# A hybrid decoder layer on eight cores: more staging buffers for x, earlier sample-cache loads, residual loads on another queue, and a narrower last token piece

## The chip, the cores and the metric

The kernel runs on all 8 cores of one Trainium2 chip. Each core computes half of one prompt (1024 tokens, with 128 tokens of halo in front) and 4 of the 32 sample tokens. The cores do not talk to each other. Times are device microseconds (us) of the slowest core.

Most executions of one kernel agree within 0.3%. Some executions fall in a slow state, in which one die (cores 0 to 3, or 4 to 7) runs at a lower granted TensorE clock and takes some per cent longer, whatever the kernel. All comparisons below use fast executions alone, and so do the medians unless their row says otherwise.

## The reference, cut to what matters

```python
# D_MODEL 2048, 4 prompts x 2048 tokens, 32 sample tokens, one layer
h = rms_norm(x, norm_mix_g)
z = h @ w_in                                  # q | k | v | conv value | conv gate
q = rope(rms_norm(q)); k = rope(rms_norm(k))
a = sliding_window_attention(q, k, v)         # window 128; sample tokens read cache_k, cache_v
u = u_val * sigmoid(u_gate)
c = silu(layer_norm(causal_dwconv(u)))
x = x + concat(a, c) @ w_out                  # "residual": x is read again here
hm = rms_norm(x, norm_mlp_g)
x = x + square(relu(hm @ w_up)) @ w_down      # hidden 8192
```

## The kernel before

Five engines work side by side: PE (matmuls), DVE and ACT (elementwise work and reading results out of PSUM), POOL and SP (these mostly issue loads). Activations lie transposed: 128 features on the partitions, tokens along the free dimension. There are 1028 real tokens on a core (1024 prompt and 4 sample), padded to `NM = 1032` and cut into three pieces of 344 columns (`PM`), so that a matmul covers 344 columns.

Every operation goes through a helper (`mm`, `tt`, `ts`, `act`, `cp`, `dma`), and each helper is one source line in the profile. In the kernel before, L613 is a matmul, L577 a DVE tensor-tensor operation, L590 a DVE scaling, L573 an ACT activation, L595 an ACT copy and L560 a load. With the change, all these numbers are higher by 3. The helper records dependencies. At build time `P.schedule()` then fixes the order on each engine with a simple model, taking program order as the priority. At run time each engine works strictly in its order.

The stages, with their times on core 0, are: x and the key/value projection (0 to 56 us), statistics, k, v and q (to 134 us), the convolution inputs with attention between them (to about 310), the output projection with the convolution's layer norm inside it (to about 440), and the MLP (to the end).

The start. x comes in 16 chunks of 128 features:

```python
XST = [sb(O_A + 16384 + 4640 * i, F32, (HW,)) for i in range(4)]       # 4 staging buffers
xd = []
for kc in range(16):
    xs_ = XST[kc % 4]
    xd.append(dma("sp", xs_(), R(xt_d[kc]), "xst%d" % (kc % 4)))
    dma("pool", WKV(kc), R(wkv_d[kc]), "wkv%d" % kc, after=[xd[max(kc - 3, 0)]] if kc >= 2 else [])
    if kc == 6:                      # loads of the rotary tables
        dma("sp", CSE(), R(cse_d), "cse", after=[xd[3]])
        dma("sp", TB(p=(0, 32)), R(tab_d...), "tab", after=[xd[3]])
    if kc == 10:                     # six times: PE spreads a table piece, ACT copies it out
        cp("act", BD(), CSE((0, 128)))
        cp("act", GQK(), CSE((256, 260)))
        for j, tb in enumerate((COS, SIN)):
            for a, b in ((0, 388), (388, 776), (776, 1160)):
                pb = ps_f32(7, 1, (b - a,))
                P.group()
                mm(pb(), CSE((128, 256), p=(0, 32)), TB(j, (a, b), p=(0, 32)), True, True)
                cp("act", tb((a, b)), pb())
    ts("dve", HT(kc), xs_(), G1(kc), ALU.mult)          # DVE: scale the chunk
    act(SQX[kc % 2](), xs_(), AF.Square)                # ACT: square it (chunk 0: into SS1 itself)
    if kc >= 2:
        tt("dve", SS1(), SS1(), SQX[(kc - 1) % 2](), ALU.add)   # DVE: sum the squares
    # PE: 10 matmuls of keys and values with this chunk
```

The sample caches are loaded on POOL's queue after the first of eight convolution channels, and the next convolution weights (`wu`) follow on the same queue:

```python
for c in range(8):
    # ... six groups of matmuls for channel c, attention between them
    if c == 0:
        gate_s = [P.streams["pe"][-1]]
        dma("pool", KTS((0, SPC), (0, 2), (0, 127)), R(ckt), "cks", group=True, after=gate_s)
        dma("pool", CVB(p=(0, 127)), R(cv[:, 1:128, :].rearrange("s k d -> k s d")), "cks", ...)
    if c == 4:
        gate_xt = [P.streams["pe"][-1]]
    for _ in range(2):
        ... wu.append(wstream(wu_d[order[wnext]], "wu", 128))
```

The output projection adds each result to a residual chunk `XT(dc)`. All residual loads are on SP's queue, and 12 of them wait for the last convolution channel:

```python
def xt_load(dc):
    dma("sp", XT(dc), R(xt_d[dc][:, MC0:MC0 + NM]), "xt%d" % dc, after=gate_xt)

def wo_half(dc, half, src):
    ...
    for kc in range(8):
        for pi, (a, b) in enumerate(PM):
            mm(accb(pi, (0, PW)), lw, src(kc, (a, b)), kc == 0, kc == 7)
    tt("dve", x3(), accb((0, 3), (0, PW)), x3(), ALU.add)

gate_xt = [u4_last]
for dc in range(4, 16):
    xt_load(dc)
...
for dc in range(6, 16):                    # first half of the projection, with the
    wo_half(dc, 0, AT)                     # convolution's layer norm between
    if dc - 6 < 8:
        ln_chunk(dc - 6)                   # two DVE operations and one ACT operation
for dc in range(16):                       # second half, and the square for the next norm
    wo_half(dc, 1, CT)
    norm2(dc)
```

In the last column block of the down-projection, the three token pieces of one accumulation finish together and are then added and stored one after the other:

```python
for i in range(n):
    for pi, (a, b) in enumerate(PM):
        mm(accb(pi, (0, PW)), wd[i](dc), hid(i % GFF, (a, b)), i == 0, i == n - 1)
if last and dc == 15:
    for pi, (a, b) in enumerate(PM):
        tt("dve", x3(pi), accb(pi, (0, PW)), x3(pi), ALU.add)
        dma("sp", R(yt[...]), XT(dc, (a, min(b, NO))), ...)
```

## Time and profile before

| | before |
|---|---|
| time, median of 6 runs, one of them slow | 1352.19 us (1349.49 to 1595.09) |
| span of cores 0 to 7 in the profile | 1350.0, 1340.4, 1342.8, 1345.9, 1345.3, 1347.0, 1339.4, 1344.4 us |
| end of DVE's last scaling of x (A), mean of cores | 57.2 us (54.3 to 60.4) |
| start of the convolution inputs on PE (B), mean | 135.5 us |
| from B to the start of the last PE group (E), mean | 1150.4 us |
| from E to the end, mean | 58.5 us |

A, B and E are marks that I set in the timelines of all eight cores. E is the last row of PE's timeline, which starts a new row after an idle time of over 0.15 us; it is the same matmul in every run, the 362nd from the end.

The head of the page gives the span and the busy time of each engine, with its share of the span:

```profile
span 1350.0 us, 22872 instructions; the slowest of 8 cores (1339.4 to 1350.0 us)
PE 1310.1 (97%) x9253; PEld 842.0 (62%) x9253; DVE 702.1 (52%) x853; ACT 290.6 (22%) x441; POOL 111.4 (8%) x199
```

PE is the bound. The chain of waits of core 0 (start, length, what) shows the steady state of the MLP, 384 matmuls in 56.25 us, or 146.5 ns per matmul of 344 columns:

```profile
507.28 56.25 PE psum L613 x384
...
563.56 56.26 PE psum L613 x384
```

Gains can therefore only come from places where PE idles or runs at a low clock, and from narrower matmuls. There are three such places.

*The start.* The table by stretches of core 0 has the columns: stretch and its length, then busy time and number of instructions of PE, PE weight loads, DVE, ACT and POOL, then granted clock, DMA share and GB/s.

```profile
40.00:44.00 4.00, 4.00 (x10) 1.53 (x10) 0.66 (x2) 2.12 (x3) 0.31 (x1) 0.50 0.71 182
44.00:48.00 4.00, 2.78 (x16) 1.34 (x14) 4.00 (x5) 2.66 (x3) 0.53 (x1) 0.80 0.79 184
48.00:52.00 4.00, 3.33 (x21) 1.81 (x20) 4.00 (x5) 1.95 (x3) 0.86 (x2) 1.00 0.92 266
```

From 40 to 44 us the DMA engines are busy only 0.71 of the time, and DVE works only 0.66 of 4 us. The timelines of ACT (first line) and DVE (the others) on core 0 show why; the bracket is the idle time before an instruction and what ended it:

```profile
41.88 0.48 ACT L595 COPY arena<-psum 128x384 f32<-128x384 f32 x1 [3.36 <-PE psum L613]
...
38.09 1.37 DVE L577 TENSOR_TENSOR arena<-arena 128x1160 f32<-128x1160 f32 x1 [3.60 <-ACT arena L573]
43.53 1.37 DVE L577 TENSOR_TENSOR arena<-arena 128x1160 f32<-128x1160 f32 x1 [3.34 <-ACT arena L573]
...
54.86 0.82 DVE L590 TENSOR_SCALAR arena<-arena 128x1160 bf16<-128x1160 f32 x1
```

ACT's copy of a rotary table piece waits for PE, whose chunk matmuls ahead of the table matmul run at clock 0.5. ACT's next square stands behind that copy, and DVE's sum waits for the square. Call this the table stall. After 43.53 us DVE runs without a wait, 2.01 us a chunk.

*The sample caches.* POOL's timeline on core 0 shows the issues, and the view of one tile the time from issue to landing, first for the value cache (`cv`), then for the convolution weights (`wu`):

```profile
152.12 0.89 POOL L560 DMA_DIRECT2D arena<-ckt  x1 [7.70 <-PE psum L613]
153.00 4.58 POOL L560 DMA_DIRECT2D arena<-cv  x1
157.57 0.56 POOL L560 DMA_DIRECT2D arena<-wu  x1
```

```profile
DMA to landing us min/median/max: 31.4/31.4/31.4
...
DMA to landing us min/median/max: 6.1/7.7/29.4
```

The value cache lands 31.4 us after its issue, and the weights behind it take 29.4 us instead of 7.7. The table by stretches (same columns) shows PE standing still, and then working at half clock:

```profile
184.00:186.00 2.00, 0.00 (x0) 0.00 (x0) 0.00 (x0) 0.00 (x0) 0.00 (x0) 0.88 0.84 166
186.00:188.00 2.00, 0.76 (x3) 0.43 (x4) 0.00 (x0) 0.00 (x0) 0.00 (x0) 0.50 0.41 73
188.00:190.00 2.00, 2.00 (x8) 1.03 (x7) 0.00 (x0) 0.00 (x0) 0.00 (x0) 0.50 0.45 109
```

*The residual.* On core 0 the timelines of DVE and PE show a long wait for x, and the wait of PE that it causes:

```profile
341.36 1.23 DVE L577 TENSOR_TENSOR arena<-psum,arena 128x1032 f32<-128x1032 f32 x1 [12.27 <-DMA arena<-xt]
...
343.98 23.86 PE L613 MATMUL psum<-arena 128*128 128x344 f32 x132 [5.63 <-DVE arena L577]
368.76 922.74 PE L613 MATMUL psum<-arena 128*128 128x344 bf16 x6292 [0.91 <-DVE arena L577]
```

No other core has this wait in the profiled execution.

*The end* costs little. On core 0 three additions follow PE's last matmuls in one piece of 1.36 us:

```profile
1344.46 1.36 DVE L577 TENSOR_TENSOR arena<-psum,arena 128x344 f32<-128x344 f32 x3 [1.98 <-PE psum L613]
```

### The profile page before, as it was taken

To read this page: it belongs to the slowest core of one execution; us is meant where nothing else is said; L and a number is where in the kernel's file an instruction comes from. 1 tells how busy PE (TensorE), PEld (TensorE's weight loads), DVE (VectorE), ACT (ScalarE), POOL (GpSimd) and SP (SyncE) were. 2 spreads that over 40 slices of the span, in tenths; PEclk is the share of its full clock that TensorE was granted. 3 is DMA by queue.
4 is the path that set the end of the run, shared out by engine and by line. 5 is a ranking of instruction groups with operands and counts; after the bars stand their busy time and mean duration, and the time that the engine had idled before them with its cause. 6 is when DMAs were issued, how large, how long until landed. Compare 5 with 4: busy or idle time off the path is not lost.

```text
span 1350.0 us, 22872 instructions; the slowest of 8 cores (1339.4 to 1350.0 us)
## 1 busy us (share of the span) xinstructions
PE 1310.1 (97%) x9253; PEld 842.0 (62%) x9253; DVE 702.1 (52%) x853; ACT 290.6 (22%) x441; POOL 111.4 (8%) x199
## 2 busy tenths in 40 slices
PE   5999989999899999999999999999999999999998
PEld 2566545555466666666666666666666666666665
DVE  4666746664676335436354363543635436354333
ACT  3655646562246310000100001000010000100000
POOL 2300200000011110010000101001010010100000
PEclk9899989999899999999999999999999999999999
DMA  9990545655847693351734517335163451624123
GB/s 239 180 161 5 62 99 107 149 112 112 222 73 121 120 158 56 69 94 32 137 58 71 94 32 137 58 72 94 32 135 59 72 94 32 126 53 73 17 106 146
DMA packets 57667, 130.58 MB, mean 97 GB/s; under 512 B 19108, under 2 KB 22692, under 8 KB 57508
## 3 DMA queue, kind: packets, MB, share of 16 engines
q0 software_dynamic: 38880, 90.74, 40.2%
q1 hardware_dynamic: 18684, 38.38, 9.4%
q8 instruction: 75, 1.23, 0.4%
q14 instruction: 28, 0.23, 0.1%
HBM read 202.31 MB, written 10.35 MB: 158 GB/s over the span
## 4 chain that ended last, share of the span: by engine, by line
PE 90%; DMA 6%; DVE 1%; SPq 1%; issue 1%; ACT 0%; POOL 0%; DVEq 0%; ACTq 0%; POOLq 0%
PE psum L613 90%; DMA arena<-xt 2%; DMA arena<-wu 2%; DVE arena L577 1%; SPq L877 1%; DMA arena<-wkv 1%; DMA arena<-arena 0%; POOL arena L560 0%; ACT arena L573 0%; DVE arena L590 0%; SPq L560 0%; ACT arena L595 0%; DVEq L384 0%; DVEq L374 0%; ACTq L374 0%
## 5 line engine op out<-in xcount | busy, mean ns | idle before, releaser
L613 PE MATMUL psum<-arena 128*128 128x344 bf16 (+6 forms) x9253 | 1310.1, 316 | 34.5 <-DMA arena<-wkv 15.1
L613 PEld LDWEIGHTS psum<-arena 128*128 128x128 bf16 (+2 forms) x9253 | 842.0, 99 | 502.3 <-issue 91.4
L577 DVE TENSOR_TENSOR arena<-psum,arena 128x1032 f32<-128x1032 f32 (+7 forms) x367 | 385.0, 1060 | 283.0 <-PE psum L613 263.5
L577 DVE TENSOR_TENSOR arena<-arena 128x516 bf16<-128x516 bf16 (+13 forms) x431 | 305.4, 735 | 343.5 <-ACT arena L573 325.9
L573 ACT ACTIVATE arena<-psum 128x512 bf16<-128x512 f32 (+8 forms) x173 | 124.6, 739 | 819.4 <-PE psum L613 809.1
L573 ACT ACTIVATE arena<-arena 128x352 f32<-128x352 f32 (+9 forms) x194 | 138.7, 730 | 90.2 <-DVE arena L577 70.8
L560 POOL DMA_DIRECT2D arena<-wup x64 | 33.8, 529 | 391.8 <-PE psum L613 391.8
L560 POOL DMA_DIRECT2D arena<-wdn x64 | 33.9, 529 | 384.7 <-PE psum L613 383.8
L573 ACT ACTIVATE arena<-psum,arena 128x344 f32<-128x344 f32 (+6 forms) x58 | 31.8, 575 | 68.7 <-PE psum L613 68.7
L590 DVE TENSOR_SCALAR arena<-arena 128x1160 bf16<-128x1160 f32 (+2 forms) x25 | 18.9, 756 | 13.2 <-DMA arena<-xt 12.2
L560 POOL DMA_DIRECT2D arena<-wo x16 | 11.3, 704 | 136.8 <-PE psum L613 136.8
L560 POOL DMA_DIRECT2D arena<-wu x16 | 8.5, 532 | 141.3 <-PE psum L613 138.4
L560 POOL DMA_DIRECT2D arena<-wkv x16 | 9.1, 567 | 35.0 <-DMA arena<-xt 34.1
L560 POOL DMA_DIRECT2D arena<-wq x16 | 9.1, 614 | 8.3 <-DMA arena<-xt 8.3
L573 ACT ACT_TABLE_LOAD x3 | 3.8, 1283 | 8.8 <-DMA arena<-xt 7.4
L595 ACT COPY arena<-psum 128x388 f32<-128x388 f32 (+1 forms) x6 | 2.9, 481 | 11.1 <-PE psum L613 11.1
L560 POOL DMA_DIRECT2D arena<-cv x1 | 4.6, 4576 | 0.0
L597 DVE COPY arena<-arena 128x4 f32<-128x4 f32 (+1 forms) x11 | 3.8, 356 | 0.4
L605 POOL MEMSET arena<- 128x32 f32 x1 | 0.1, 124 | 42.6 <-PE psum L613 42.6
L590 DVE TENSOR_SCALAR arena<-psum 128x388 bf16<-128x388 f32 (+1 forms) x3 | 1.7, 560 | 1.9 <-PE psum L613 1.8
L601 DVE TENSOR_REDUCE arena<-arena 128x4 f32<-128x124 f32 x8 | 2.2, 278 | 0.5
L595 ACT CAST arena<-arena 128x128 bf16<-128x128 f32 (+2 forms) x6 | 1.5, 300 | 0.5 <-DMA arena<-cse 0.5
(9 smaller groups left out, 3.8 us busy)
## 6 DMA issues: line engine op xcount, KB each, us to landing
arena<-wdn POOLq DMA_DIRECT2D x64, 512.0 KB, 9.4
arena<-wup POOLq DMA_DIRECT2D x64, 512.0 KB, 6.1
arena<-xt SPq DMA_DIRECT2D x16, 580.0 KB, 9.1
arena<-arena SPq DMA_DIRECT2D x128, 65.8 KB, 4.0
arena<-xt SPq DMA_DIRECT2D x16, 516.0 KB, 17.7
arena<-wu POOLq DMA_DIRECT2D x16, 512.0 KB, 7.7
arena<-wo POOLq DMA_DIRECT2D x16, 512.0 KB, 7.1
yt<-arena SPq DMA_DIRECT2D x15, 514.0 KB, 3.9
```

Of the source, the lines that this page charges most:

```text
L560: return P.add(eng, lambda e: e.dma_start(out=out.ap, in_=in_.ap), reads=[in_], writes=[out], key=key, group=group, final=final, after=aft ...
L573: return P.add("act", lambda e: e.activation(out=out.ap, in_=in_.ap, func=func, bias=b, scale=s), reads=rd, writes=[out], cost=cost("act", ...
L577: return P.add(eng, lambda e: e.tensor_tensor(out=out.ap, in0=in0.ap, in1=in1.ap, op=op), reads=[in0, in1], writes=[out], cost=cost(eng, o ...
L590: return P.add(eng, lambda e: e.tensor_scalar(out=out.ap, in0=in0.ap, scalar1=a, scalar2=b, op0=op0, **kw), reads=rd, writes=[out], cost=c ...
L595: return P.add("act", lambda e: e.copy(out=out.ap, in_=in_.ap), reads=[in_], writes=[out], cost=cost("act", out, [in_]))
L597: return P.add(eng, lambda e: e.tensor_copy(out=out.ap, in_=in_.ap), reads=[in_], writes=[out], cost=cost(eng, out, [in_]))
L601: return P.add("dve", lambda e: e.tensor_reduce(out=out.ap, in_=in_.ap, axis=AX.X, op=ALU.add), reads=[in_], writes=[out], cost=(size(in_) ...
L605: return P.add(eng, lambda e: e.memset(out.ap, val), writes=[out], cost=cost(eng, out, []))
L613: return P.add("pe", lambda e: e.matmul(out.ap, lhsT.ap, rhs.ap, start=start, stop=stop), reads=[lhsT, rhs], writes=[out], cost=c)
L877: last = P.add("sp", (lambda src=src, dst=dst: (lambda e: e.dma_start(out=dst.ap, in_=src.ap)))(), reads=[src], writes=[u4()] if i == 0 el ...
```

## The change

It has five parts. (1) x gets eight staging buffers, with six loads in flight, so that its loads run ahead through the table stall. (2) The sample caches are loaded while q is computed, ahead of the convolution. (3) Twelve of the residual loads go to ACT's queue and are issued one by one in step with the output projection, whose column order changes to fit. (4) The last token piece has 340 columns instead of 344. (5) The last column block of the down-projection finishes its token pieces one after the other.

```diff
+PN = [(0, 344), (344, 688), (688, 1028)]
-    XST = [sb(O_A + 16384 + 4640 * i, F32, (HW,)) for i in range(4)]
+    XST = ([sb(O_A + 16384 + 4640 * i, F32, (HW,)) for i in range(4)]
+           + [sb(O_E + 9280 + 4640 * i, F32, (HW,)) for i in range(2)]
+           + [sb(O_G + 4640 + 4640 * i, F32, (HW,)) for i in range(2)])
@@ loop over the chunks of x
-        xs_ = XST[kc % 4]
-        xd.append(dma("sp", xs_(), R(xt_d[kc]), "xst%d" % (kc % 4)))
-        dma("pool", WKV(kc), R(wkv_d[kc]), "wkv%d" % kc, after=[xd[max(kc - 3, 0)]] if kc >= 2 else [])
+        xs_ = XST[kc % 8]
+        xd.append(dma("sp", xs_(), R(xt_d[kc]), "xst%d" % (kc % 8), after=[xd[kc - 6]] if kc >= 6 else []))
+        dma("pool", WKV(kc), R(wkv_d[kc]), "wkv%d" % kc, after=[xd[max(kc - 4, 0)]] if kc >= 2 else [])
@@ before the q projection
+    wu_d3 = P.streams["pool"][-1]
@@ after it (and removed from "if c == 0" of the convolution loop)
+    gate_s = [wu_d3]
+    dma("pool", KTS((0, SPC), (0, 2), (0, 127)), R(ckt), "cks", group=True, after=gate_s)
+    dma("pool", CVB(p=(0, 127)), R(cv[:, 1:128, :]...), "cks", group=True, after=gate_s)
@@ output projection
-        dma("sp", XT(dc), R(xt_d[dc][:, MC0:MC0 + NM]), "xt%d" % dc, after=gate_xt)
+        dma("sp" if dc < 4 else "act", XT(dc), R(xt_d[dc][:, MC0:MC0 + NM]), "xt%d" % dc, after=gate_xt)
-    gate_xt = [u4_last]
-    for dc in range(4, 16):
-        xt_load(dc)
+    DCO = list(range(4)) + list(range(8, 16)) + list(range(4, 8))
+    gate_xt = []
+    xt_more(3)                       # three loads ahead
+    ... xt_more(n): issues the next n residual loads, in the order of DCO
+    def wo_first(i):
+        wo_half(DCO[i], 0, AT)
+        gate_xt = [P.streams["pe"][-1]]
+        xt_more(1)                   # one more after each column block
@@ all large matmuls after attention
-            for pi, (a, b) in enumerate(PM):
-                mm(accb(pi, (0, PW)), lw, src(kc, (a, b)), kc == 0, kc == 7)
+            for pi, (a, b) in enumerate(PN):
+                mm(accb(pi, (0, b - a)), lw, src(kc, (a, b)), kc == 0, kc == 7)
@@ down-projection
+            if last and dc == 15:
+                steps = [(i, pi) for pi in range(3) for i in range(n)]
... (weight pairs, norm2 and the up-projection follow the new order and width)
```

More of the change, by code (lines that the diff above doesn't have):

```diff
@@ L824, in build_program @@
     dma("sp", FS((0, 8), (0, SPC), (0, 30)), R(sct), "fs", after=[wqd[15]])
+    gate_s = [wu_d3]
+    dma("pool", KTS((0, SPC), (0, 2), (0, 127)), R(ckt), "cks", group=True, after=gate_s)
+    dma("pool", CVB(p=(0, 127)), R(cv[:, 1:128, :].rearrange("s k d -> k s d")), "cks", group=True, after=gate_s)
+    for s in range(SPC):
+        dma("sp", CVB(s, p=(127, 128)), VB_S(p=(s, s + 1)), "cvs", group=True)
     CC = sb(O_B, F32, (8, NM))
@@ L975, in build_program @@
     wo2 = []
+    PAIRS = [0, 1, 4, 5, 6, 7, 2, 3]
     def wo_load(half, pair):
@@ L997, in build_program @@
         u4_last = u_done(c)
-        if c == 0:
-            gate_s = [P.streams["pe"][-1]]
-            dma("pool", KTS((0, SPC), (0, 2), (0, 127)), R(ckt), "cks", group=True, after=gate_s)
-            dma("pool", CVB(p=(0, 127)), R(cv[:, 1:128, :].rearrange("s k d -> k s d")), "cks", group=True, after=gate_s)
-            for s in range(SPC):
-                dma("sp", CVB(s, p=(127, 128)), VB_S(p=(s, s + 1)), "cvs", group=True)
         if c == 4:
@@ L1010, in build_program @@
             else:
-                wo2.append(wo_load(0, len(wo2)))
+                wo2.append(wo_load(0, PAIRS[len(wo2)]))
     dma("sp", R(uf_d), Ref(UF.ap.rearrange("p a b -> p (a b)"), UF().rngs), "uf", final=True)
@@ L1015, in xt_load @@
     def xt_load(dc):
-        dma("sp", XT(dc), R(xt_d[dc][:, MC0:MC0 + NM]), "xt%d" % dc, after=gate_xt)
+        dma("sp" if dc < 4 else "act", XT(dc), R(xt_d[dc][:, MC0:MC0 + NM]), "xt%d" % dc, after=gate_xt)
     for dc in range(4):
         xt_load(dc)
-    wo_left = [(0, p) for p in range(len(wo2), 8)] + [(1, p) for p in range(8)]
+    wo_left = [(0, p) for p in PAIRS[len(wo2):]] + [(1, p) for p in PAIRS]
     def wo_half(dc, half, src):
@@ L1062, in build_program, with xt_more @@
     conv_sums(6)
-    gate_xt = [u4_last]
-    for dc in range(4, 16):
-        xt_load(dc)
-    for dc in range(3):
-        wo_half(dc, 0, AT)
+    DCO = list(range(4)) + list(range(8, 16)) + list(range(4, 8))
+    xt_next = [4]
+    def xt_more(n):
+        for _ in range(n):
+            if xt_next[0] < 16:
+                xt_load(DCO[xt_next[0]])
+                xt_next[0] += 1
+    gate_xt = []
+    xt_more(3)
+    def wo_first(i):
+        nonlocal gate_xt
+        wo_half(DCO[i], 0, AT)
+        gate_xt = [P.streams["pe"][-1]]
+        xt_more(1)
+    for i in range(3):
+        wo_first(i)
     conv_job(7, 0)
@@ L1070, in build_program @@
     conv_sums(7)
-    for dc in range(3, 6):
-        wo_half(dc, 0, AT)
+    for i in range(3, 6):
+        wo_first(i)
     ln_stats()
-    for dc in range(6, 16):
-        wo_half(dc, 0, AT)
-        if dc - 6 < 8:
-            ln_chunk(dc - 6)
+    for i in range(6, 16):
+        wo_first(i)
+        if i - 6 < 8:
+            ln_chunk(i - 6)
     HM = sb(O_B, BF16, (16, NM))
@@ L1081, in build_program, with norm2 @@
     SS = sb(O_F + 8256, F32, (NM,))
-    def norm2(dc):
-        sq = SQ2[dc % 2]
+    def norm2(dc, i):
+        sq = SQ2[i % 2]
         act(HM(dc), XT(dc), AF.Identity, scale=G2(dc))
         act(sq(), XT(dc), AF.Square)
-        if dc == 0:
+        if i == 0:
             cp("dve", SS(), sq())
@@ L1092, in build_program @@
     gate_wdn = []
-    for dc in range(16):
+    for i, dc in enumerate(DCO):
         wo_half(dc, 1, CT)
-        if dc >= 8 and dc % 2 == 0:
+        if i >= 8 and i % 2 == 0:
             gate_wdn.append([P.streams["pe"][-1]])
-        norm2(dc)
+        norm2(dc, i)
     RS2f = sb(O_H + 8256, F32, (NM,))
@@ L1128, in up_group @@
             for kc in range(16):
-                for pi, (a, b) in enumerate(PM):
-                    mm(accb(pi, (0, PW)), w(kc), HM(kc, (a, b)), kc == 0, kc == 15)
+                for pi, (a, b) in enumerate(PN):
+                    mm(accb(pi, (0, b - a)), w(kc), HM(kc, (a, b)), kc == 0, kc == 15)
             if nextup[0] < NFF:
@@ L1159, in down_groups @@
             n = len(gs) * GFF
-            for i in range(n):
+            steps = [(i, pi) for i in range(n) for pi in range(3)]
+            if last and dc == 15:
+                steps = [(i, pi) for pi in range(3) for i in range(n)]
+            for i, pi in steps:
                 hid = HID[gs[i // GFF] % 2]
-                for pi, (a, b) in enumerate(PM):
-                    mm(accb(pi, (0, PW)), wd[i](dc), hid(i % GFF, (a, b)), i == 0, i == n - 1)
+                a, b = PN[pi]
+                if last and dc == 15 and i == 0:
+                    P.group()
+                mm(accb(pi, (0, b - a)), wd[i](dc), hid(i % GFF, (a, b)), i == 0, i == n - 1)
             x3 = sub3(XT, dc, PW)
```

## The prediction

> **What bounds it now.** On the page PE is busy 1310.1 of 1350.0 us. In the timeline PE never idles over 0.2 us after 369 us: 384 matmuls take 56.25 us again and again, 146.5 ns per 344 columns. The Trainium skill (TensorE: Matmul & The Clock Gate, "Back-to-back issue gap") has N / 2.4 + 2.5 = 145.8 ns; the trace agrees. Gains lie in idle places and columns.
>
> 1. *Start* (tables by stretch, timeline). The DMA share is about 1.0 from 4 to 40 us, then 0.7 (0.2-0.7 on cores 3, 4, 5, 7) until 48 us, as x waits for its four buffers. DVE waits 2-5 us three times for ACT, whose in-order copies of the rotary tables wait for PE chunks at clock 0.5; then DVE runs back to back at 2.01 us a chunk. The last chunk's matmuls start at 55.8 us on cores 0, 1, 2, 6 and at 59.1-60.5 on the others. Arrivals at the undisturbed 2.4 us pace would put the last x at 49-50 us. Eight buffers let loads run through the stall but don't remove it, and may push the table work later, with fewer slow chunks between its steps. Estimate: last chunk at 52.5 us; gain 3 us on early cores, 6-8 on late ones, possibly zero.
>
> 2. *Sample caches* (waits, DMA issues). The value-cache load issues at 153 us and lands 31.4 us later; the weight load queued behind it takes 29.4 us instead of 7.7. PE waits 5.6-6.8 us for it on every core, then runs at clock 0.5 for about 5.5 us (2.8 us lost). Issued after the fourth conv weight load, it falls in 104-150 us, where DMA share is 0.00-0.14. Gain 8.5-9.5 us on every core: the surest large term.
>
> 3. *Residual loads.* Only core 0 idles: DVE waits 12.3 us for x, PE 5.6 us for DVE, then half clock: 8.4 us, on the slowest core alone. ACT gets 12 issues, about 0.6 us each, where it has room. A new wait at the first up-projection is possible (chunks 4-7 are now normalised last, used 2-3 us in): up to 1 us.
>
> 4. *340 columns.* 2304 matmuls (256 + 1024 + 1024) lose 4 columns, 1.67 ns each: 3.8 us.
>
> 5. *Tail.* Two of the three last additions and output issues move under PE: 0.9 us.
>
> **Sum.** Per core, span minus start gain, gap, columns and tail gives 1323-1326 us; core 0 falls in with the rest. Time is 1.6 us above the slowest span: **1328 us**, range **1320 to 1337**, 1.8% faster: faster by over 2% 0.29, within 2% 0.69, slower 0.02.
>
> **Right if:** the PE wait for conv weights at 182-192 us is gone on all cores and the clock stays 1.0 there; the value-cache load lies within 90-140 us; core 0 has no wait for x near 340 us; the stretch of 384 falls by 0.21 us (128 narrower pieces); DMA share stays near 1.0 until the last x; last-chunk matmuls start at 50-54 us on all cores.
>
> **Wrong if:** the table stall stays in place and pins DVE, so the last chunk still starts at 55-59 us (4 to 6 us worse); six x loads in flight delay the kv weights and PE waits for those; ACT blocks at a residual load whose buffer isn't free and holds up the convolution's evictions; residual loads come late on another core. If the tables no longer interrupt DVE, the start gains 2 us more and crosses 2%.

## The result, and the profile after

| | before | after |
|---|---|---|
| time, median of all runs | 1352.28 us (20 runs, 1347.35 to 1595.09) | 1338.26 us (10 runs, 1337.72 to 1591.01) |
| the same, fast runs alone | 1352.19 us (18 runs) | 1338.17 us (6 runs) |
| ratio of fast runs | | 0.9897, 95% interval 0.9879 to 0.9914 |
| slowest and mean span in the profile | 1350.0, 1344.4 | 1337.9, 1336.1 |
| A, mean | 57.2 | 57.9 |
| B, mean | 135.5 | 138.0 |
| B to E, mean | 1150.4 | 1139.9 |
| E to the end, mean | 58.5 | 58.2 |

Ratios here and below are the mean time of one kernel's fast runs over that of the other's of the same rounds, so they are not quite the ratio of the medians that I quote.

The kernel is about 1.0% faster, and the prediction's range ended at 1337. All of the gain lies after B. The start became 2.5 us longer, where it should have become shorter.

The head of the page after:

```profile
span 1337.9 us, 22849 instructions; the slowest of 8 cores (1334.6 to 1337.9 us)
PE 1306.0 (98%) x9253; PEld 842.2 (63%) x9253; DVE 701.6 (52%) x853; ACT 291.0 (22%) x441; POOL 113.3 (8%) x199
```

PE's busy time fell by 4.1 us, and the rest of the gain is idle time. The start on core 0, by stretches (columns as before):

```profile
40.00:44.00 4.00, 3.28 (x9) 1.55 (x8) 0.00 (x0) 1.08 (x2) 0.53 (x1) 0.50 1.07 270
44.00:48.00 4.00, 4.00 (x12) 1.35 (x11) 2.10 (x2) 0.95 (x2) 0.53 (x1) 0.50 1.01 257
48.00:52.00 4.00, 4.00 (x11) 1.49 (x10) 0.34 (x1) 2.06 (x3) 1.17 (x3) 0.50 0.95 165
```

The loads do run ahead now (DMA share 1.07, 1.01, 0.95), as predicted: the last chunk of x lands at 49.1 to 50.8 us on the eight cores, where it was 51.0 to 58.2. DVE does nothing at all from 40 to 44 us, and the clock stays at 0.5 until 53.1 us. The timelines of ACT and DVE on core 0:

```profile
49.94 0.48 ACT L598 COPY arena<-psum 128x384 f32<-128x384 f32 x1 [4.19 <-PE psum L616]
...
44.65 1.37 DVE L580 TENSOR_TENSOR arena<-arena 128x1160 f32<-128x1160 f32 x1 [4.92 <-ACT arena L576]
51.66 1.37 DVE L580 TENSOR_TENSOR arena<-arena 128x1160 f32<-128x1160 f32 x1 [4.91 <-ACT arena L576]
...
58.98 0.82 DVE L593 TENSOR_SCALAR arena<-arena 128x1160 bf16<-128x1160 f32 x1
```

The table stall ends 8.1 us later on this core (51.66 instead of 43.53). Behind it come four scalings of 2.01 us each, where it was six, which gives back 4.0 us. The last scaling is thus 4.1 us later. On core 3 it goes the other way: the last stalled step starts at 48.15 us before and 47.54 after, and with four scalings behind it instead of six the last one ends 4.7 us earlier. Over the eight cores the last stalled step starts at 45.0 us before and 49.8 after, always with six scalings behind it before and four after. Later by 4.74, less two scalings of 2.01, is later by 0.72 us, and the mean of A did move by 0.71. The tables' loads fit the delay. They are issued at about 16 us in both kernels, and the tile's view on core 0 gives their time to landing, before:

```profile
DMA to landing us min/median/max: 11.6/11.6/11.6
```

And the same view of the kernel after:

```profile
DMA to landing us min/median/max: 16.6/16.6/16.6
```

More chunks of x are now ahead of them. On all eight cores the larger of the two table loads lands at 26.0 to 28.0 us before and at 31.9 to 33.7 after. In e1 below, which goes back to the old loads of x, it lands at 26.8 to 28.2 again, and the last stalled step is back at 44.6 us on the mean.

The sample caches, POOL's timeline and PE's stretch on core 0:

```profile
98.25 0.89 POOL L563 DMA_DIRECT2D arena<-ckt  x1 [14.80 <-DMA arena<-wu]
99.14 4.58 POOL L563 DMA_DIRECT2D arena<-cv  x1
...
148.97 0.56 POOL L563 DMA_DIRECT2D arena<-wu  x1 [12.98 <-PE psum L616]
```

```profile
184.00:186.00 2.00, 2.00 (x15) 1.28 (x14) 0.92 (x3) 2.00 (x6) 0.00 (x0) 1.00 0.29 71
186.00:188.00 2.00, 2.00 (x16) 1.27 (x13) 1.52 (x4) 1.67 (x4) 0.53 (x1) 1.00 0.63 117
```

The cache load is issued at 99 us, lands 27.5 us later, and nothing queues behind it until 149 us. PE works through the place where it stood still, at clock 1.00.

The residual: the long waits of DVE and PE near 340 us are gone on all cores. PE's timeline on core 0 has a longer wait at the layer norm instead, 2.03 us, where it was 0.91. DVE's timeline shows what it waits for:

```profile
145.77 212.92 PE L616 MATMUL psum<-arena 128*128 128x356 bf16 x1852 [0.23 <-DVE arena L580]
360.72 525.75 PE L616 MATMUL psum<-arena 128*128 128x344 bf16 x3594 [2.03 <-DVE arena L580]
886.78 391.00 PE L616 MATMUL psum<-arena 128*128 128x344 bf16 x2674 [0.31 <-DVE arena L580]
...
354.76 4.66 DVE L580 TENSOR_TENSOR arena<-arena 128x1032 f32<-128x1032 f32 x4
359.35 1.22 DVE L580 TENSOR_TENSOR arena<-psum,arena 128x1032 f32<-128x1032 f32 x1
```

The wait of 0.31 us at 886 us, in the MLP, is new as well; the section on 344 columns comes back to it. At the layer norm, four layer-norm operations stand ahead of the addition that frees a PSUM buffer for PE. On cores 3, 4 and 5 the same wait is followed by a stretch at half clock. By stretches, core 3:

```profile
356.00:358.00 2.00, 0.23 (x2) 0.00 (x0) 2.00 (x2) 2.00 (x3) 0.71 (x1) 1.00 0.00 0
358.00:360.00 2.00, 1.75 (x8) 1.01 (x9) 2.00 (x3) 1.09 (x2) 0.00 (x0) 0.65 0.71 84
360.00:362.00 2.00, 2.00 (x9) 1.06 (x8) 2.00 (x3) 0.59 (x1) 0.00 (x0) 0.50 0.95 177
```

These three cores need 1141.0 us from B to E and the other five 1139.3, so the half clock costs 1.7 us there. That fits its length, which is 3.41 us on each of the three. In the repeat of this kernel below it hits two cores (1 and 3).

The narrower piece and the end: the chain of waits of core 1 (the slowest) and its DVE timeline.

```profile
495.49 56.05 PE psum L616 x384
```

```profile
1329.95 0.52 DVE L580 TENSOR_TENSOR arena<-psum,arena 128x344 f32<-128x344 f32 x1 [0.65 <-PE psum L616]
1331.11 0.52 DVE L580 TENSOR_TENSOR arena<-psum,arena 128x344 f32<-128x344 f32 x1 [0.64 <-PE psum L616]
```

A stretch of 384 matmuls takes 0.20 us less, and only one addition of 0.52 us is left behind PE, where three took 1.36 us.

### The profile page after: what moved, and what is told of

Same layout as the page of the kernel before. It is cut to its first block, busy times and chain, and to the rows that moved or that the text cites. A ratio compares the mean times of both kernels' runs of the same rounds, so it can differ in the third digit from the quotient of the medians.

```text
span 1337.9 us, 22849 instructions; the slowest of 8 cores (1334.6 to 1337.9 us)
## 1 busy us (share of the span) xinstructions
PE 1306.0 (98%) x9253; PEld 842.2 (63%) x9253; DVE 701.6 (52%) x853; ACT 291.0 (22%) x441; POOL 113.3 (8%) x199
## 3 DMA queue, kind: packets, MB, share of 16 engines
q8 instruction: 75, 1.23, 0.4%
## 4 chain that ended last, share of the span: by engine, by line
PE 95%; DMA 2%; DVE 1%; issue 1%; ACT 0%; SPq 0%; DVEq 0%; ACTq 0%
PE psum L616 95%; DMA arena<-tab 1%; DVE arena L580 1%; DMA arena<-xt 1%; ACT arena L576 0%; SPq L563 0%; ACT arena L598 0%; DVE arena L593 0%; DVEq L375 0%; ACTq L375 0%; SPq L375 0%
## 5 line engine op out<-in xcount | busy, mean ns | idle before, releaser
L616 PE MATMUL psum<-arena 128*128 128x344 bf16 (+8 forms) x9253 | 1306.0, 315 | 25.0 <-DMA arena<-wkv 15.6
L616 PEld LDWEIGHTS psum<-arena 128*128 128x128 bf16 (+3 forms) x9253 | 842.2, 99 | 488.5 <-issue 82.7
L576 ACT ACTIVATE arena<-psum 128x512 bf16<-128x512 f32 (+7 forms) x173 | 124.7, 741 | 807.1 <-PE psum L616 806.6
L593 DVE TENSOR_SCALAR arena<-arena 128x1160 bf16<-128x1160 f32 (+2 forms) x25 | 15.6, 626 | 12.7 <-DMA arena<-xt 11.8
```

The lines of the kernel that those rows point to most:

```text
L576: return P.add("act", lambda e: e.activation(out=out.ap, in_=in_.ap, func=func, bias=b, scale=s), reads=rd, writes=[out], cost=cost("act", ...
L593: return P.add(eng, lambda e: e.tensor_scalar(out=out.ap, in0=in0.ap, scalar1=a, scalar2=b, op0=op0, **kw), reads=rd, writes=[out], cost=c ...
L616: return P.add("pe", lambda e: e.matmul(out.ap, lhsT.ap, rhs.ap, start=start, stop=stop), reads=[lhsT, rhs], writes=[out], cost=c)
```

## The experiments

All runs had five rounds and gave correct results. Three batches ran, each on one chip with its own runs of the kernel before:

| run | what it is | A | B | B to E | E to end | mean span | median of fast runs | ratio to before (95%) |
|---|---|---|---|---|---|---|---|---|
| before | | 57.2 | 135.5 | 1150.4 | 58.5 | 1344.4 | 1352.19 | 1 |
| after | | 57.9 | 138.0 | 1139.9 | 58.2 | 1336.1 | 1338.17 | 0.9897 (0.9879–0.9914) |
| e1_four_buffers | after, old x loads | 57.0 | 135.2 | 1140.0 | 57.3 | 1332.6 | 1336.76 | 0.9881 (0.9864–0.9897) |
| e2_tables_first | after, tables before x | 50.1 | 132.0 | 1139.8 | 57.7 | 1329.4 | 1333.35 | 0.9852 (0.9838–0.9867) |
| e3_tables_first_four | both | 52.8 | 131.5 | 1139.3 | 57.7 | 1328.4 | 1332.33 | 0.9845 (0.9832–0.9859) |
| e5_cache_alone | before, cache loads moved | 55.1 | 134.2 | 1142.6 | 57.9 | 1334.8 | 1343.82 | 0.9935 (0.9921–0.995) |
| e4_old_residual | after, old residual | 57.4 | 137.5 | 1141.0 | 56.6 | 1335.0 | 1343.35 | 0.9944 (0.9917–0.997) |
| e6_old_tail | after, old tail | 57.7 | 137.5 | 1139.7 | 59.4 | 1336.6 | 1339.03 | 0.9914 (0.9891–0.9937) |
| e7_344 | after, 344 columns | 57.7 | 137.4 | 1142.8 | 57.8 | 1338.0 | 1342.33 | 0.9939 (0.9916–0.9962) |
| e8_five_in_flight | e2, five loads in flight | 50.0 | 130.3 | 1138.7 | 58.0 | 1327.0 | 1331.44 | 0.9857 (0.9824–0.989) |
| c_after_again | after, unedited | 58.1 | 137.7 | 1140.0 | 58.8 | 1336.5 | 1339.51 | 0.9884 (0.9852–0.9916) |
| e9_norm_later | e8, layer norm one block later | 51.2 | 132.3 | 1138.8 | 58.7 | 1329.7 | 1333.23 | 0.9835 (0.9806–0.9863) |
| e10_kv_ahead | e9, kv weights one chunk earlier | 51.3 | 132.9 | 1138.8 | 58.6 | 1330.3 | 1332.80 | 0.9833 (0.9804–0.9861) |

The marks are means over the eight cores of one profiled execution, except e8's, whose profile fell in the slow state: there they are of the six undisturbed cores. The fast medians of the kernel before in the three batches were 1353.51 (e1, e2, e3, e5), 1351.86 (e4, e6, e7, e8) and 1355.74 (c, e9, e10). In every single case the difference from the kernel before is below 2%.

My theory after reading the two traces was that the table stall still sets DVE's pace at the start, now from a later point. Its rivals were that the eight buffers themselves do harm (by crowding out the weights, or by the changed order of matmuls), and that the start was never worth what I had put on it.

### Four buffers again

```diff
-    XST = ([... 4 at O_A] + [... 2 at O_E] + [... 2 at O_G])
+    XST = [sb(O_A + 16384 + 4640 * i, F32, (HW,)) for i in range(4)]
-        xs_ = XST[kc % 8]   ... after=[xd[kc - 6]] if kc >= 6 else []   ... wkv after xd[kc - 4]
+        xs_ = XST[kc % 4]   ... (no after)                              ... wkv after xd[kc - 3]
```

> The changed kernel with four staging buffers for x and the old gates of the kv weights; all else as changed. PE's order then has the eight q matmuls between the last x chunk's statistics and the first spread again. Theory A (the copies of the rotary tables on ACT, waiting for PE, hold DVE, so that eight buffers bring nothing; and eight buffers reorder what follows): the mean over cores of the end of the last scaling of x on DVE stays within 1.5 us of 57.9, the stretch from there to the first conv matmuls falls from 80.1 to about 78.1 us, the time is 1 to 3 us shorter than that of the changed kernel. Rival B (eight buffers do shorten the start, and something else was lost there): the last scaling ends 3 us or more later than 57.9 us and the time is longer than that of the changed kernel.

A hardly moves (57.9 to 57.0), but B is reached 2.8 us earlier: 135.2 instead of 138.0. The eight buffers, with the gates that go with them, therefore make the start worse by about 2.5 us. Most of that (1.8 us) lies behind the last scaling, between A and B. The time itself moves by less than the intervals resolve (0.9881 against 0.9897, in different batches), so the marks carry this reading. They repeat: in the five profiles with eight buffers and the tables in their old place (after, its repeat, e4, e6, e7) the mean of B is 137.4 to 138.0 us, and in the three with the old loads of x (before, e1, e5) it is 134.2 to 135.5. From B to E this run gains nothing on the mean because seven of its eight cores fall to half clock at the layer norm; the eighth needs 1138.5 us. On four of its eight cores the last stall is one of 4.98 or 4.99 us; the kernel before had four such cores as well (4.91 to 4.92 us), and six scalings follow in both.

Why is the stretch from A to B longer? With the other x dependencies the build-time order of the matmuls also changed. In the kernel before, eight matmuls of q fill the place between the statistics matmuls and the first that spreads the statistics over the partitions. In the kernel after they are gone from there, and PE waits 0.46 and 0.30 us for ACT at 64 to 65 us. In the old order A to B takes 78.0 us, or 79.7 on cores that fall to half clock around 61 to 66 us. In the new order it takes 79.0 us, or 80.0 to 80.6 with half clock. The order thus costs 0.94 us, and a half-clock stretch up to 1.67. One core of eight was hit in the kernel before, and one in this run. In the kernel after it was six. I can't attribute that frequency to a part of the change, because e5 has the old order and its mean from A to B is 79.1.

### Tables ahead of x

```diff
+    dma("sp", CSE(), R(cse_d), "cse")
+    dma("sp", TB(p=(0, 32)), R(tab_d...), "tab")
+    ... the two copies and the six table steps, unchanged, ahead of the loop
     xd = []
     for kc in range(16):
-        if kc == 6:   ... (the two loads)
-        if kc == 10:  ... (the copies and the six steps)
```

> The changed kernel with the two loads of the rotary tables put ahead of the first x and the table matmuls and copies ahead of the first chunk. Theory A: no chunk on DVE waits for an ACT that waits for PE any more, the loads set the pace (about 2.4 us a chunk), the last scaling of x ends at 50 to 53 us instead of 57.9, and the time is 5 to 7 us shorter than that of the changed kernel (about 1332). Rival C (the start is bound by DMA or by DVE's own work): the last scaling stays at 56 us or later, less than 2 us gained.

A falls from 57.9 to 50.1 us, more than the prediction had asked of the eight buffers (52.5). The long waits of DVE for ACT (1.8 to 3.7 us) now come between 16 and 26 us, with 12 or 13 scalings still to follow, at a time when x is still arriving. DVE's timeline on core 0 has none left after 30 us: until the last scaling, which ends at 50.2 us, the longest waits are these.

```profile
44.64 1.37 DVE L580 TENSOR_TENSOR arena<-arena 128x1160 f32<-128x1160 f32 x1 [0.54 <-ACT arena L576]
46.70 0.83 DVE L593 TENSOR_SCALAR arena<-arena 128x1160 bf16<-128x1160 f32 x1 [0.70 <-DMA arena<-xt]
...
49.35 0.82 DVE L593 TENSOR_SCALAR arena<-arena 128x1160 bf16<-128x1160 f32 x1
```

The clock is 1.00 from 24 to 60 us on this core. The stall did set the pace. Of the 7.8 us at A, 6.0 arrive at B, and the time falls by 4.8 us against after's fast median (in another batch), a little less than the 5 to 7 expected. One thing these runs do not separate: the half clock of PE (36 to 53 us on core 0 of the kernel after) went away together with the stall. At clock 1.00 the table steps of e2 come 3.9 to 4.7 us apart on DVE, where at 0.50 they came 7.0 us apart (44.65 and 51.66 above), which suggests that the clock sets part of the stall's length. What began the half clock is not shown.

### Tables ahead of x, with four buffers

The edit is that of the two runs above together.

> Tables first and four staging buffers, all else as changed. It completes the two by two. If four buffers suffice once the stall is gone, the last scaling of x ends within 1 us of that with eight buffers, 50 to 53 us. If the eight buffers are worth something by themselves, it ends 1.5 us or more later. Theory A expects the former, since four loads in flight already kept the DMA share at 1.0 before the stall; after it the stretch to the first conv matmuls should be about 78 us, so that this kernel is 2 us faster than the one with eight.

A is 52.8 us, 2.7 later than with eight buffers, so the expectation failed there. B is 131.5, no later than with eight (132.0), and the time is no longer (1332.3 against 1333.3). With the stall out of the way eight buffers do bring DVE ahead, but behind A the lead is lost: A to B takes 81.8 us in e2 and 78.7 here. In e2 PE waits 0.3 to 1.6 us at a time for key/value weights at the last chunks, and its order lacks the q matmuls, as in the kernel after; the shares of the two are not separated. So at B eight buffers gain nothing with the stall away, and with the stall in place they cost 2.5 us or so (e1). On the same chip, against e1, moving the tables gains 4.4 us of time with four buffers.

### The cache loads alone

```diff
 (on the kernel before)
+    wu_d3 = P.streams["pool"][-1]           # before q
+    gate_s = [wu_d3]                        # after q: the ckt and cv loads
-        if c == 0:  ...                     # the same loads, in the convolution loop
```

> The kernel before with the early loads of the sample caches alone; the order on PE, DVE and ACT is the same as before. Expected: the wait of PE for conv weights of 5.6 to 6.8 us and the half clock after it are gone on all cores, the stretch from the first conv matmuls to the last group falls by 8.5 to 9.5 us on every core (by 1.3 more on core 5), core 0 keeps its wait for x near 335 us, and the time falls by about 9 us, to 1343. A rival (the wait for weights moves to a later weight load): less than 5 us.

The order of PE, DVE and ACT is identical to the kernel before. On the six undisturbed cores B to E falls from about 1149.2 to 1140.7 us, that is by 8.5, and the time by 9.7 us between the medians of the fast runs and 8.7 between their means (the interval of the ratio allows 7 to 11). This one part is worth most of the whole change. The two other cores, 4 and 7, now show the residual wait that core 0 had. PE's and DVE's timeline on core 4:

```profile
336.97 22.71 PE L613 MATMUL psum<-arena 128*128 128x344 f32 x132 [6.16 <-DVE arena L577]
...
334.45 1.23 DVE L577 TENSOR_TENSOR arena<-psum,arena 128x1032 f32<-128x1032 f32 x1 [12.91 <-DMA arena<-xt]
```

### The old residual loads

```diff
-    PAIRS = [0, 1, 4, 5, 6, 7, 2, 3]
+    PAIRS = list(range(8))
-        dma("sp" if dc < 4 else "act", XT(dc), ...)
+        dma("sp", XT(dc), ...)
-    ... wo_first(i), xt_more(1)
+    gate_xt = [u4_last]
+    for dc in range(4, 16):
+        xt_load(dc)
+    ... wo_half(dc, 0, AT)
```

> The changed kernel with the residual loads as before (sync queue, first four early, twelve behind the last transposed u, output columns in order 0 to 15, old order of the weight pairs); the rest as changed. Theory D (the new loads changed the order on DVE at the layer norm, one more layer-norm operation of 1.15 us ahead of an addition that PE waits for): PE's wait there falls from 2.03 to about 0.9 us and the stretch from the first conv matmuls to the last group falls from 1139.3-1141.0 to 1137.5-1138.3 us on cores without a wait for x; one or two cores, not always core 0, wait about 6 us for x near 335 us and are 8 us longer. So the mean span is about equal, but the time, that of the slowest core, is 3 to 6 us longer than that of the changed kernel. Rival (the stretch stays at 1139-1141 us: the gain was lost elsewhere).

The mean span is 1335.0 us, even a little below after's 1336.1, yet the time is 1343.4, some 4 to 5 us more than after's 1338.2 and its repeat's 1339.5. Cores 2 and 4 have the wait (PE 6.45 and 5.62 us, B to E 1147.9 and 1145.8) and core 1 a short one of 2.35 us. The undisturbed cores need 1138.5 to 1138.65 us, less than the 1139.3 of the best cores after, and their wait at the layer norm is 1.23 us (PE's timeline on core 0):

```profile
352.83 529.23 PE L616 MATMUL psum<-arena 128*128 128x344 bf16 x3618 [1.23 <-DVE arena L580]
```

That is above the 0.9 expected, and B to E misses the expected 1137.5 to 1138.3 by 0.2 to 0.4; why is not shown. Laid over the kernel after matmul by matmul, these cores are 0.8 us ahead behind this wait and still 0.6 to 0.8 at E, so the gain does lie there. Both readings matter: the wait picks some cores in each execution, so that the slowest core nearly always pays it, and the new loads cost every core about 0.8 us at the layer norm.

### The old end

```diff
-            if last and dc == 15:
-                steps = [(i, pi) for pi in range(3) for i in range(n)]
-                if last and dc == 15 and i == 0:
-                    P.group()
```

> The changed kernel with the three pieces of the last output column interleaved again. PE, DVE and all queues are otherwise the same. Prediction's sum: 0.9 us longer. From the profiles so far (end of the last PE group to the end of the span, 58.2 us with the old tail and 57.7 with the new, of which 0.2 is columns): 0.3 to 0.7 us longer, within the noise of the time; the last output issue starts about 0.7 us later after the last matmul.

E to the end is 59.4 us, against 58.2 in after, 58.8 in its repeat and 57.8 in e7 on the same chip. The time, 1339.0, can't be told from after's two medians. Over all ten profiles with the new end the mean is 57.9, over the three with the old one 58.6, of which 0.1 is the 344 columns of two of these three; single profiles spread by over 1 us (56.6 to 59.4). The issue of the last output shows the gain without this noise: it starts 1.30 us behind PE's last matmul on every core of the three runs with the old end, and 0.70 behind it on every core of the others. The new end is worth 0.60 us there. How long the last output then takes to land differs more than that from run to run.

### 344 columns

```diff
-PN = [(0, 344), (344, 688), (688, 1028)]
+PN = [(0, 344), (344, 688), (688, 1032)]
```

> The changed kernel with a last piece of 344 columns. The order on all engines is the same. If a narrower matmul saves in proportion, the repeating stretch of 384 matmuls is 56.28 us again and the kernel is 3.4 to 3.8 us longer. If part of the saving is turned into waits of PE for DVE at the layer norm, where DVE sets the pace, the wait of 2.03 us shrinks by 0.2 to 0.5 us and the difference is nearer 3 us.

B to E is 1142.75 us on all cores alike (1142.66 to 1142.83), against 1139.3 on the undisturbed cores of after: 3.45 us. The wait at the layer norm is 2.17 us here and 2.03 in after, so it doesn't come from the narrower piece, and 0.14 of the difference is this wait: the columns are worth 3.3 us. The repeat of the kernel after agrees: its wait is 2.21 us, its undisturbed cores need about 1139.5, and the difference is again 3.2 to 3.3.

This run also brings out a cost that the marks hide. From the 2400th matmul behind B, just behind the start of the MLP, to E, every core of the kernel after needs 844.0 us, and so, within 0.1, do the other runs with 340 columns and six loads of x in flight (the repeat, e2, e4, e6). With four buffers or five loads in flight (e1, e3, e8, e9, e10) the same matmuls take 843.1 to 843.3 us. With 344 columns it is 846.7 to 846.9 here, and 845.8 to 846.1 with the old loads of x (before, e5). So the new loads of x cost 0.9 us in the MLP as well, hundreds of microseconds after x was loaded. Core 1 of e8 gains it on core 0 of the kernel after at three places (613, 886 and 1011 us of core 0) at which PE waits for DVE in the one and not in the other; the middle one is the 0.31 us shown above. The builds differ in the order of the first matmuls. How that reaches the MLP I have not traced.

### Tables first, five loads in flight

```diff
 (on e2)
-        xd.append(dma(..., after=[xd[kc - 6]] if kc >= 6 else []))
+        xd.append(dma(..., after=[xd[kc - 5]] if kc >= 5 else []))
```

> Tables first, eight buffers, and five x loads in flight instead of six, which is enough for the order on PE after the last chunk to have the eight q matmuls ahead of the first spread again. Theory E (the 2 to 3.7 us more from the last scaling to the first conv matmuls come from that order: PE is idle or does single-column matmuls for about 4 us and its clock falls to half): the stretch falls from 81.8 to about 78.3 us, the last scaling stays at 50 to 51.5 us, and the time is about 3 us shorter than with six in flight, near 1330. Rival (the extra time is DMA contention of the weights for q): the stretch stays above 80.

With five loads in flight the build-time order puts the q matmuls back between the statistics. A to B falls only from 81.8 to 80.4 us. B comes at 130.3, the earliest of all runs, and the three fast runs took 1331.2 to 1331.6 us. By what was written beforehand (78.3 expected, above 80 for the rival, contention of the weight loads for q) the rival did better. But the means differ by less than the spread of single cores (79.7 to 81.9 here, 79.8 to 83.1 in e2), so the order may be part of the loss between A and B, and is not all of it; contention was not tested. With the tables first PE is itself behind DVE when the last chunk arrives (on five of the six undisturbed cores its last long wait for key/value weights is 0.9 to 1.7 us), so A no longer marks the point from which PE's work follows.

### The unedited kernel once more

> The changed kernel once more, unedited, as a yardstick on the same chip as the next two and to see how much the start varies. Expected: 1338 us within 1 us, the last scaling of x at a mean of 57 to 58.5 us over the cores (55.5 to 60 on single ones), the first conv matmuls at 137.5 to 138.5 us, PE's wait at the layer norm 2.0 us on all cores. If the start were 3 us or more off the 57.9 of the first profile, the comparison of starts with the experiments would not hold.

All marks repeat within 0.6 us, and the fast median within 1.4 (1339.5, half a microsecond above what was expected). PE's wait at the layer norm is 2.2 us on all cores and not 2.0: the same program differs by 0.2 us there from one profile to the next, so a difference of 0.2 us between such waits is not evidence of a cause.

### The layer norm one column block later

```diff
 (on e8)
-        if i - 6 < 8:
-            ln_chunk(i - 6)
+        if 0 <= i - 7 < 8:
+            ln_chunk(i - 7)
```

> Tables first, eight buffers, five in flight, and the layer norm's chunks started one output column later, which takes one layer-norm operation from ahead of the addition that PE waits for; PE, ACT, POOL and SP have the same order as in the run with five in flight. Theory D: PE's wait at 352-354 us falls from 2.03 us to about 0.9, cores that lost 1.7 us to a half clock after it lose nothing, the stretch from the first conv matmuls to the last group falls by 1 us to about 1137.5, the time by about 1 us, to 1330. Rival (DVE's total work at the layer norm sets the pace and the order doesn't matter): the stretch stays at 1138.4 us or the wait shows at a later column.

PE's timeline on core 0:

```profile
351.56 17.16 PE L616 MATMUL psum<-arena 128*128 128x344 bf16 x117 [1.01 <-DVE arena L580]
369.92 30.38 PE L616 MATMUL psum<-arena 128*128 128x344 bf16 x208 [1.21 <-ACT arena L576]
```

The wait for DVE falls to 1.0 us, but a wait of 1.2 us for ACT's normalised chunk appears 18 us later. B to E stays at 1138.8 (e8: 1138.7). The wait was moved and not removed, which fits the rival: what DVE and ACT have to do around the layer norm sets the pace there, and not the place of one addition. One part of the expectation held: no core fell to half clock at the layer norm, here or in e10.

### Key/value weights one chunk earlier

```diff
 (on e9)
-        dma("pool", WKV(kc), ..., after=[xd[max(kc - 4, 0)]] if kc >= 2 else [])
+        dma("pool", WKV(kc), ..., after=[xd[max(kc - 5, 0)]] if kc >= 2 else [])
```

> As the run before with each kv weight load released one x chunk earlier. In the run with five in flight PE still waited 1 to 1.7 us for kv weights at the last chunks while DVE was ahead. If that is what holds the start now, the first conv matmuls start 0.5 to 1.5 us earlier than in the run before (130.2 us there) and the time falls by as much; if the loads as a whole hold it, x comes later by what the weights gain and nothing changes (within 0.5 us).

Nothing is gained: B is 132.9 against 132.3, the time 1332.8 against 1333.2. Gating these weights less doesn't bring them sooner: the last of them is issued 2.7 us earlier on the mean and lands at 51.1 to 52.9 us, against 51.0 to 52.9 in e9. The Trainium skill ("DMA: Bandwidth & Descriptors", section "Issuing engines are not separate DMA queues") says that loads issued from different engines run on the same 16 DMA engines and interleave. That fits a start in which the DMA share is already 1.0 (on core 0 of e2 between 1.01 and 1.07 from 24 to 60 us), so that an earlier issue only waits longer. No run here varies the number of bytes, so this stays a reading.

## Why the prediction was right or wrong

The measured time is 10 us above the predicted 1328 and 1.3 us above the range (1.2 by the fast median). In the profiled execution the prediction's 1323 to 1326 us a core stand against a mean span of 1336.1.

**The start: wrong, and this is the step that failed.** The prediction said "Eight buffers let loads run through the stall but don't remove it, and may push the table work later, with fewer slow chunks between its steps. Estimate: last chunk at 52.5 us". The first half happened. But the table work moved later *without* fewer slow chunks between its steps: two waits of 4.9 us still follow each other on core 0. DVE, and not the arrival of x, then set the end of the stage: the last x landed at 49.1 to 50.8 us, as the prediction's 49 to 50 had it, but its matmuls started at 55.7 to 59.9. The arithmetic that holds on the mean of all cores is: the last stalled step (45.0 us before, 49.8 after) plus the scalings behind it (six, then four, at 2.01 us). The estimate took the arrival of the last x as the bound and added a little. It should have followed DVE from the stall's end. I had named this failure under "wrong if" ("the table stall stays in place and pins DVE", 4 to 6 us worse), and gave it too little weight. Measured, A is 0.7 us later instead of 4.7 earlier (57.2 to 52.5; the prediction's mark, the start of the last chunk's matmuls, lies about 0.15 us behind A), and the changed order and half clock behind it add 1.8. Together B is 7.2 us later than predicted. Runs e1, e2 and e3 show it: taking the stall away gives 7.8 us at A with the same eight buffers, and the number of buffers alone gives none at B. The last sentence of the prediction, that 2 us more would come if the tables no longer interrupted DVE, was right in kind: that is the lever, though no run reached 2%.

**The sample caches: right.** Predicted 8.5 to 9.5 us on every core; e5 shows 8.5 us on undisturbed cores, and about 9 us of time. The Trainium skill ("TensorE: Matmul & The Clock Gate", section "What's actually happening") has the clock fall to half after at least one idle window of about 3.4 us and return after about 3.4 us of activity. The trace before agrees in the fall (PE idle for 6.36 us, then clock 0.50); the return took 5.1 us of work on this core and 3.4 to 5.7 on the eight, 4.6 on the mean. The prediction took 5.5 us and 2.8 lost; with 2.3 lost, and a mean wait of 6.2 us, the sum is the 8.5 that e5 shows.

**The residual loads: the gain right, its place and its price wrong.** "Only core 0 idles" read one execution as a property of that core. In e5 it is cores 4 and 7, in e4 cores 2 and 4. The gain in time (4 to 5 us in e4) is there nevertheless, since the slowest core decides; that it came out although its reason was misread was partly luck. The price was not foreseen: 2.03 instead of 0.91 us at the layer norm (e4 gives back 0.8 of this), and on three cores half clock behind it, 1.7 us each. The new wait that the prediction had feared, at the first up-projection, was not what came.

**340 columns: right, a little too large.** Predicted 3.8 us, measured 3.3 in B to E (e7) and about 0.2 more behind E. The stretch of 384 shrank by 0.20 us against the predicted 0.21. The prediction checked the form of N / 2.4 + 2.5 ns from the skill's section "Back-to-back issue gap" on 344 columns, where 146.5 ns agrees with 145.8, and took its 1.67 ns for 4 columns from the slope; 0.20 us over 128 narrower pieces is 1.6. The section gives this form for an isolated matmul and says that at large N it is too high for a stream; here the stream of 384 ran at it.

**The end: right in kind, too large.** Predicted 0.9 us; the last output is issued 0.60 us sooner behind PE's last matmul (e6), as 1.36 us of additions became 0.52 on DVE. In E to the end the gain is not resolved (58.6 to 57.9, with a spread of over 1).

In sum the mean span is some 11.6 us above the middle of the predicted 1323 to 1326. About 7.2 of it is the start, 0.5 the caches, 0.3 the columns, 1.8 the layer norm (1.1 us more wait, and the half clock on three of eight cores, 0.6 on the mean), 0.9 the waits in the MLP that came with the new loads of x, and 0.7 the end (E to the end was to fall by 1.1 us with the columns there, and fell by 0.4). That is 11.4 us. Each term is a mean over one profiled execution, so the remaining 0.2 says nothing. Open are the path from the loads of x to the MLP, and how often a core falls to half clock, behind the last chunk of x and at the layer norm.

The tables-first versions beat both kernels: 1332.3 us with four buffers (e3), 1331.4 to 1333.3 with eight (e8, e10, e9, e2), against 1338.2 to 1339.5 for the kernel after. Their ratios to the kernel before, 0.9833 to 0.9857, have overlapping intervals, so none of them is shown to be the best. Simplest is e3. It needs no extra buffer at all.

## What to carry to other kernels

More buffers did not help here, because the loads were not what ended last. Where in-order copies on one engine hold up another, follow the held-up engine from the end of its last stall, count what it still has to do, and move the interrupting work out of the way before deepening the prefetch. A wait that one core shows in one profile can belong to any core in the next execution, so cost it on the slowest core of several runs. A slow load is best issued where nothing that is needed soon stands behind it on its queue.

## What the Trainium skill lacked or had wrong

- "DMA: Bandwidth & Descriptors" ("Why a DMA increments its semaphore by 16 and not by 1") says that a 127-partition load is spread over one engine, with an exception for some direct copies issued by software, which get all 16. The value cache here (127 partitions, issued from POOL) takes 27.5 us in the kernel after while the DMA share is 0.07 from 115 to 130 us, close to one engine of 16 (0.06). The key cache beside it (128 partitions, the same 254 KB) lands in 4.3 to 5.4 us. The page doesn't let one tell beforehand which case a load falls in; no run here shows which engines were used.
- No page that I found gives the cost of standing behind such a load on the same queue: the convolution weights took 29.4 us instead of a median of 7.7, and PE waited 6.4 us for them.
- "TensorE: Matmul & The Clock Gate" ("What's actually happening") ties half clock to an idle window of about 3.4 us. In the kernel after, the wait at the layer norm, 2.03 us on core 0, was followed by a clock of 0.50 on cores 3, 4 and 5 and not on the other five. Between 36 and 52 us core 0 stayed at 0.50 with PE busy 3.3 to 4.0 of every 4 us. From 43.55 us it ran without a pause of over 0.15 us, and the clock came back only at 53.1, where the page has about 3.4 us of sustained work. In the traces of both kernels every stretch at half clock that ends within the kernel lasts 3.41 us or a whole multiple of it (up to 20.48), which fits the page's window, and the 1.7 us lost are half of one. But the page gives no way to tell which short waits will cost the clock.
